# Sums of the down weights moved behind the prompt attention and issued by POOL, with other orders of work around both MLP products, in a one-core decoder layer in split fp32

## The chip, the core and the metric

The kernel runs on one core of one Trainium2 chip. The metric is the device time of one execution in microseconds (us), the median of several runs. The engines are named as in the profile: PE (TensorE, matmuls), DVE (VectorE), ACT (ScalarE), POOL (GpSimd) and SP (the engine that only issues DMAs here).

## The reference

One decoder layer is computed for 1024 prompt tokens with 16 meta tokens ahead of them, and for 8 sequences of 8 new tokens with their caches: L = 1088 output columns, D_MODEL = 1024, D_FF = 4096.

```python
u = _rmsnorm(h, norm_mix)
z = u @ w_in + b_in                      # 1024 -> 6144: pool, conv (2x), q, k, v, three gates
y_a, pool_state = _pool_mixer(a_in, ...) # causal mean pooling, group maps
y_b, conv_state = _conv_mixer(c_in, ...) # GLU, depthwise conv of 31, LayerNorm, silu, product
o, k_state, v_state = _attention_prompt(...) / _attention_sample(...)
y_c = o @ w_attn_out
merged = gates[:, :, 0] * y_a + gates[:, :, 1] * y_b + gates[:, :, 2] * y_c
h = h + merged @ w_out
u2 = _rmsnorm(h, norm_mlp)
h = h + jnp.square(jax.nn.relu(u2 @ w_up)) @ w_down
y = _rmsnorm(h, norm_final)              # and the new pool, conv, key and value states
```

## The kernel before

Every fp32 product is made of three matmuls in a reduced fp32 form: high part by high part, low by high, high by low. A weight tile of 128x1024 is loaded (`wraw`), its high part is rounded off by ACT (`whi`, L90) and the rest made by DVE (`wlo`, L91). Activations lie transposed, with 1088 columns; a tile of output rows is made in three chunks of columns (400, 320 and 368 in the later tiles), 24 matmuls each.

The stages, with their place in the span of the profile: a head to about 77 us; the in-projection, 48 tiles in a loop over `ti` (77 to 724); the products for attention and pooling (724 to 850), the convolution branch (850 to 884) and the merge, W_out (884 to 977); the MLP's up product (977 to 1327) and its down product (1327 to 1679); and the last norm. Both MLP products are made by a scheme with seven products in place of eight (of Strassen's kind), which wants sums of weight blocks and sums of activation blocks.

In the loop over `ti` each chunk is followed by `slot()`, which takes one piece of work from the queue `attq` (attention, norms, loads) and up to two from `dveq` (the 31 convolution taps, each an L444 and an L446 on DVE, among them). Prompt attention runs this way as 64 slices from about 110 to 515 us; then come the sample attention (about 500 to 600 us) and the tiles of the gates. `store()` hands a DMA store to SP at the next slot. Each engine runs its instructions in the order in which the program writes them, so what a queue pops where sets the order.

The pieces that the change touches:

- **Sums of the down weights.** `down_sums` adds and subtracts blocks of `w_down` on POOL (32 times 128x1024, L989), in 8 groups of 4; `sum_load` loads the four blocks of a group (`wd`), and each sum is stored to `sumD` in DRAM, to be read by the down product from 1366 us on. In the kernel before one sum is popped with each of 32 attention slices, the next group's loads go out behind the third sum of a group, and SP issues loads and stores. POOL's other work there is the low part of q (`uq`, L558), on which the attention's score matmuls (`qk`, L569) wait.
- **`tail_slices`** loads and splits the attention's output (`ol`, DVE) for the product that follows.
- **The LayerNorm of the convolution branch** adds four tiles on POOL to `lacc` (L486, L488); PE reads `lacc` (L496, `px<-lacc,ones`) within the gate tiles.
- **Up seam** (977 to 1010 us). The last output rows of W_out are evicted (`h`, L1389), scaled, combined to `t` and split. POOL makes sums of up-weight blocks (`s`, L1266 to L1272), combinations (`t`, L1360, L1361) and the sums of squares of h (`sqa`, L1293, after an ACT square, L1292); from the last `sqa` come the norm's scales, by matmuls with ones (`px<-ones,sqa`, L242), `mv` and `diag` on DVE (L1420, L1421, L248). `start_steps` lists the pieces popped at the first steps of the up product, in that order.
- **Down seam** (1327 to 1355 us). `op_store` stores combined activation blocks (`opT`, `opB`) that the down product loads again (`ld`); the last pair (j = 15) is made while the down product has begun. `W` holds the weight tiles: with `paged` the raw tile and both parts lie in pages of their own, else in rings of two.
- **Last product.** `residual` (L1658, L1657, POOL) adds the old h and the row terms to the output rows; `done` holds that and the sums of squares for the last norm.

## Time and profile before

| | us |
|---|---|
| median of 3 runs (lowest to highest) | 1692.72 (1691.68 to 1692.99) |
| the profiled execution, whole | 1691.97 |
| its span in the trace | 1689.9 |
| PE busy | 1655.2 |
| DVE / ACT / POOL busy | 1091.6 / 747.8 / 513.7 |

The profiled execution spends 2.07 us outside its span. Its time lies between the lowest and the highest of the three runs. The clock that the chip grants PE is given as a share (1.00 is the full 2.4 GHz).

### The profile page before, as it was taken

The page shows a single profiled execution, that of the slowest core. Times are in us where ns is not written, and L with a number is a line of the kernel's source. Part 1 is how long each engine was busy: PE and PEld are TensorE (multiplying, and loading weights), DVE is VectorE, ACT ScalarE, POOL GpSimd, SP SyncE. Part 2 cuts the span into 40 slices and gives each one's busy share as a digit, 9 for nine tenths or more (in the row PEclk, how much of TensorE's full clock was granted, in tenths as well). Part 3 has the DMA queues.
Part 4 walks back from the last instruction along what each step waited for, and adds up shares of the span by engine and source line. Part 5 has one row for each costly group of instructions (what it writes and reads, how often), then busy time and mean ns, then how long its engine had stood idle before and what let it go on. Part 6 is the DMA issues. An engine that isn't in the chain of part 4 may idle for free.

```text
span 1689.9 us, 29160 instructions
## 1 busy us (share of the span) xinstructions
PE 1655.2 (98%) x11552; PEld 1620.4 (96%) x11552; DVE 1091.6 (65%) x1745; ACT 747.8 (44%) x1424; POOL 513.7 (30%) x358
## 2 busy tenths in 40 slices
PE   8999999999999999999999989999999899999997
PEld 7999899998999999999989989999999899999997
DVE  7787878888887666344464575565555644467565
ACT  6536666466665342364243443333333433333341
POOL 1022333133340002212342555555555300013330
PEclk9999999999999999999999999999999999999999
DMA  5255554263545353354243413444444655556552
GB/s 203 65 112 158 156 163 155 72 179 128 160 126 164 108 193 108 101 192 144 79 161 121 152 61 128 143 144 143 144 144 163 250 198 180 183 174 204 203 184 90
DMA packets 124157, 250.79 MB, mean 148 GB/s; under 512 B 33427, under 2 KB 64628, under 8 KB 124020
## 3 DMA queue, kind: packets, MB, share of 16 engines
q1 hardware_dynamic: 124020, 248.92, 44.5%
q8 instruction: 91, 1.49, 0.4%
q14 instruction: 46, 0.38, 0.1%
HBM read 168.52 MB, written 80.36 MB: 147 GB/s over the span
## 4 chain that ended last, share of the span: by engine, by line
PE 77%; DVE 11%; ACT 7%; issue 3%; DMA 1%; POOL 1%; SPq 0%; DVEq 0%; ACTq 0%; POOLq 0%
PE pm L148 9%; PE pm L149 9%; PE pm L150 9%; PE m L1632 6%; PE m L1628 6%; PE m L1630 6%; PE m L1450 6%; PE m L1452 6%; PE m L1453 6%; PE pn L148 3%; PE pn L150 3%; PE pn L149 3%; ACT lg L589 2%; DVE y L446 2%; DVE y L444 2%
## 5 line engine op out<-in xcount | busy, mean ns | idle before, releaser
L148 PE MATMUL pm<-uh,whi 128*128 128x320 f32 (+3 forms) x1008 | 339.0, 336 | 6.5 <-ACT uh L324 6.5
L149 PE MATMUL pm<-ul,whi 128*128 128x320 f32 (+3 forms) x1008 | 333.0, 330 | 0.7 <-DVE ul L325 0.6
L150 PE MATMUL pm<-uh,wlo 128*128 128x320 f32 (+3 forms) x1008 | 332.4, 330 | 0.0
L1628 PE MATMUL m<-oph,whi 128*128 128x272 f32 (+2 forms) x896 | 259.4, 290 | 4.8 <-ACT whi L90 4.8
L1632 PE MATMUL m<-oph,wlo 128*128 128x272 f32 (+2 forms) x896 | 259.0, 289 | 1.2 <-DVE wlo L91 1.2
L1630 PE MATMUL m<-opl,whi 128*128 128x272 f32 (+2 forms) x896 | 258.6, 289 | 0.0
L91 DVE TENSOR_TENSOR wlo<-wraw,whi 128x1024 fp32r<-128x1024 f32 (+1 forms) x127 | 172.6, 1359 | 112.2 <-ACT whi L90 112.2
L90 ACT ACTIVATE whi<-wraw 128x1024 fp32r<-128x1024 f32 (+1 forms) x127 | 130.2, 1026 | 203.6 <-PE m L1630 139.3
L148 PEld LDWEIGHTS pm<-uh,whi 128*128 128x128 f32 x1008 | 191.1, 190 | 7.9 <-ACT uh L324 6.5
L149 PEld LDWEIGHTS pm<-ul,whi 128*128 128x128 f32 x1008 | 191.2, 190 | 3.3 <-DVE ul L325 2.9
L150 PEld LDWEIGHTS pm<-uh,wlo 128*128 128x128 f32 x1008 | 190.9, 189 | 0.2
L1628 PEld LDWEIGHTS m<-oph,whi 128*128 128x128 f32 x896 | 169.4, 189 | 5.1 <-ACT whi L90 5.1
L1632 PEld LDWEIGHTS m<-oph,wlo 128*128 128x128 f32 x896 | 169.3, 189 | 2.0 <-DVE wlo L91 2.0
L1630 PEld LDWEIGHTS m<-opl,whi 128*128 128x128 f32 x896 | 169.5, 189 | 0.0
L444 DVE SCALAR_TENSOR_TENSOR y<-ext,vec,y 128x1024 f32<-128x1024 f32 x120 | 158.7, 1323 | 0.0
L1450 PE MATMUL m<-bch,whi 128*128 128x272 f32 x448 | 130.5, 291 | 3.2 <-DVE mv L1420 2.9
L1450 PE MATMUL m<-bch,wlo 128*128 128x272 f32 x448 | 129.4, 289 | 1.9 <-ACT s L1573 1.1
L1452 PE MATMUL m<-bcl,whi 128*128 128x272 f32 x448 | 130.1, 290 | 0.0
L1453 PE MATMUL m<-bch,whi 128*128 128x272 f32 x448 | 130.0, 290 | 0.0
L558 POOL TENSOR_TENSOR uq<-q,uq 128x128 fp32r<-128x128 f32 x64 | 34.9, 566 | 310.3 <-ACT uq L557 301.6
L1452 PE MATMUL m<-bcl,wlo 128*128 128x272 f32 x448 | 129.0, 288 | 0.0
L1453 PE MATMUL m<-bch,wlo 128*128 128x272 f32 x448 | 128.8, 288 | 0.0
(363 smaller groups left out, 3887.6 us busy)
## 6 DMA issues: line engine op xcount, KB each, us to landing
wraw<-w_in SPq DMA_DIRECT2D x46, 512.0 KB, 4.1
opT<-d SPq DMA_DIRECT2D x64, 272.0 KB, 2.5
ld<-opT SPq DMA_DIRECT2D x32, 544.0 KB, 4.6
wd<-w_down SPq DMA_DIRECT2D x32, 512.0 KB, 5.6
sumD<-wd SPq DMA_DIRECT2D x32, 512.0 KB, 3.5
wraw<-sumD SPq DMA_DIRECT2D x32, 512.0 KB, 3.6
gt<-gD SPq DMA_DIRECT2D x24, 544.0 KB, 4.5
ld<-opB SPq DMA_DIRECT2D x23, 544.0 KB, 4.8
```

Of the source, the lines that this page charges most:

```text
L90: self.nc.scalar.activation(hi, r, AF.Copy)
L91: self.late.append(lambda lo=lo, r=r, hi=hi: self.nc.vector.tensor_tensor(lo, r, hi.bitcast(F32), ALU.subtract))
L148: PE.matmul(ps, lhsT=wh[k], rhs=xh, start=first and i == 0, stop=False)
L149: PE.matmul(ps, lhsT=wh[k], rhs=xl, start=False, stop=False)
L150: PE.matmul(ps, lhsT=wl[k], rhs=xh, start=False, stop=last and i == n - 1)
L444: V.scalar_tensor_tensor(y[:, :NP], e[:, k:k + NP], w, y[:, :NP], ALU.mult, ALU.add)
L1450: PE.matmul(ps, lhsT=wh, rhs=xh, start=first and k == 0, stop=False, skip_group_check=True)
L1452: PE.matmul(ps, lhsT=wh, rhs=xl, start=False, stop=False, skip_group_check=True)
L1453: PE.matmul(ps, lhsT=wl, rhs=xh, start=False, stop=k == 3, skip_group_check=True)
L1628: PE.matmul(ps, lhsT=wh[:, w], rhs=xh[:, r], start=k == 0, stop=False, skip_group_check=True)
L1630: PE.matmul(ps, lhsT=wh[:, w], rhs=xl[:, r], start=False, stop=False, skip_group_check=True)
L1632: PE.matmul(ps, lhsT=wl[:, w], rhs=xh[:, r], start=False, stop=k == 15, skip_group_check=True)
```

## The change

The parts, by number:

1. The sums of the down weights leave the attention slices. They are popped in the tile loop from ti = 31 to 42 by a condition that spreads 32 over 36 chunks; POOL issues the loads and the stores itself, and the next group's loads go out behind the fourth sum. `tail_slices` goes to the front of `attq` at ti = 43.
2. One empty piece of work goes into `attq` ahead of the convolution branch's output loop.
3. W_out's last three chunks take their PSUM banks in another order.
4. `sum_pair(0, 3)` stands ahead of `last_t(1)`.
5. `start_steps`: the two last squares of h are popped with the first and third piece, and their adds are popped by themselves, on DVE, as the seventh and eighth; the norm's scales (`rs[0]`) come after these.
6. `op_store` for j = 15 goes into `attq`, one store a slot.
7. In the last product the weights of mp = 1 to 3 have paged parts and a raw ring of two, and those of mp = 0 rings alone; before, mp = 0 to 2 lay in pages altogether and mp = 3 in rings.
8. `residual(2mp+1, LO)` is queued at the sixth product; the last product's queue holds the sums of squares of rows 1, 3 and 5, the two halves of the last norm's first part, and the sum of squares of row 7.

```diff
+SUM0, SUM1 = 31, 43
...
-        if paged:
+        if paged is True or paged and tag != "wraw":
...
                 if cur:
                     units[n].exps()
-                    sumq.pop(0)()
...
                 attq.extend(sample_slices())
                 attq.append(lambda: wide.append(0))
-                attq.extend(tail_slices())
...
             for b in range(4):
-                SP.dma_start(wdt[g][b], I["w_down"][g // 2, g % 2, b])
+                G.dma_start(wdt[g][b], I["w_down"][g // 2, g % 2, b])
...
                 G.tensor_tensor(t[o], t[a], t[b], op)
-                store(d[n], t[o])
-                if n == 2:
+                G.dma_start(d[n], t[o])
+                if n == 3:
                     sum_load(g + 1)
...
-        if ti == NHEAD:
+        if ti == SUM0:
             sum_load(0)
             for g in range(8):
                 sumq.extend(down_sums(g))
+        if ti == SUM1:
+            attq[:0] = tail_slices()
...
             slot(1, NDVE[0] if attq else NDVE[1])
+            if SUM0 <= ti and sumq and                     len(sumq) * 3 * (SUM1 - SUM0) > 32 * (3 * (SUM1 - ti) - 1 - ci):
+                sumq.pop(0)()
...
+    attq.append(lambda: None)
     for m in range(8):
         wh, wl = weights(WCO + m, 4)
...
-            for t, n in (("px", 3), ("qk", 2), ("qk", 2))]
+            for t, n in (("qk", 2), ("qk", 2), ("px", 3))]
...
+    sum_pair(0, 3)
     last_t(1)
-    sum_pair(0, 3)
...
     def op_store(x, j, t):
-        store(opD[x, j // 2][:, (j % 2) * HL:(j % 2) * HL + HL], t)
+        go = lambda: store(opD[x, j // 2][:, (j % 2) * HL:(j % 2) * HL + HL], t)
+        if j < 15:
+            go()
+        else:
+            attq.append(go)
...
-                                  (n == mp == hf == 0) or (n == NPROD - 1 and mp < 3))
+                                  n == mp == hf == 0 or
+                                  ("out" if n == NPROD - 1 and mp else False))
...
-        def s1():
-            sq_add(7, h7.pop())
-            sq_add(3, h3.pop())
-            comb_split("T3", 3)
-
...
-        return [lambda: comb_split("B22", 3), s1, lambda: comb_split("B21", 3), s3,
-                rs[0], idle, rs[1], s6]
+        sq = []
+
+        def s0(x, h):
+            comb_split(x, 3)
+            sq.append(page("sqt"))
+            A.activation(sq[-1][:, :L], h.pop()[:, :L], AF.Square)
+
+        def add():
+            q = sq.pop(0)
+            V.tensor_tensor(sqa[:, :L], sqa[:, :L], q[:, :L], ALU.add)
+        return [lambda: s0("B22", h3), lambda: comb_split("T3", 3), lambda: s0("B21", h7), s3,
+                idle, add, add, rs[0], idle, rs[1], s6]
...
+            elif n == 5:
+                attq.append(lambda m=2 * mp + 1: residual(m, LO))
...
-    for mp in range(4):
-        attq.extend(done(2 * mp + 1, LO))
-    attq.extend(fin[0] + fin[1])
+    sqs = [lambda m=m: sum_sq(m, LO) for m in (1, 3, 5, 7)]
+    attq.extend(sqs[:3] + fin[0] + fin[1] + sqs[3:])
```

**POOL from the last attention slices to the LayerNorm's first add.** Before, a sum stands behind each pair of `uq`; these are the last two, and the `lacc` adds follow the sample attention's memsets:

```order
L989 TENSOR_TENSOR wd<-wd 128x1024
L558 TENSOR_TENSOR uq<-q,uq 128x128 x2
L989 TENSOR_TENSOR wd<-wd 128x1024
L677 MEMSET sqh 128x1024
L678 MEMSET sql 128x1024
L677 MEMSET sqh 128x1024
L678 MEMSET sql 128x1024
L486 TENSOR_TENSOR lacc<-y 128x1088
L488 TENSOR_TENSOR lacc<-lacc,y 128x1088 x2
```

Now the attention slices hold `uq` alone, and behind the last of them stand eight groups of this kind (the first is shown, `wd` with buffer numbers):

```order
L974 DMA wd_5555<-w_down 128x1024
L974 DMA wd_5556<-w_down 128x1024
L974 DMA wd_5557<-w_down 128x1024
L974 DMA wd_5558<-w_down 128x1024
L988 TENSOR_TENSOR wd_5558<-wd_5557,wd_5558 128x1024
L989 DMA sumD00_5563<-wd_5558 128x1024
L988 TENSOR_TENSOR wd_5557<-wd_5555,wd_5557 128x1024
L989 DMA sumD00_5563<-wd_5557 128x1024
L988 TENSOR_TENSOR wd_5555<-wd_5558,wd_5555 128x1024
L989 DMA sumD00_5563<-wd_5555 128x1024
L988 TENSOR_TENSOR wd_5556<-wd_5556,wd_5555 128x1024
L989 DMA sumD00_5563<-wd_5556 128x1024
```

So POOL has 64 DMAs to issue that it did not have, the first sum of a group reads the block that was asked for last, the loads of a group stand right behind the stores of the one before, and the `lacc` adds stand behind the 32nd sum. In PE's order the first matmul out of `lacc` stands 96 matmuls of the tiles (four chunks) later than before.

**POOL at the up seam.** Before (one pair's last sums and the next pair's first):

```order
L1360 TENSOR_TENSOR t_10212<-u 128x544
L1361 TENSOR_TENSOR t_10212<-u,t_10107 128x544
L1272 TENSOR_TENSOR s_10088<-wra 128x512
L1293 TENSOR_TENSOR sqa<-sqa,sqt 128x1088 x2
L1266 TENSOR_TENSOR s_10354<-wraw 128x512
L1268 TENSOR_TENSOR s_10354<-s_10354,wraw 128x512
```

Now:

```order
L1276 TENSOR_TENSOR s_10088<-wra 128x512
L1364 TENSOR_TENSOR t_10213<-u 128x544
L1365 TENSOR_TENSOR t_10213<-u,t_10107 128x544
L1270 TENSOR_TENSOR s_10350<-wraw 128x512
L1272 TENSOR_TENSOR s_10350<-s_10350,wraw 128x512
```

The last sum of the first pair has moved ahead of the two combinations, and the two adds of squares have left POOL.

**SP at the down seam.** Before:

```order
L1521 DMA ld<-opT_10240 128x1088
L222 DMA opB_10270<-cb 128x544
L222 DMA opB_10254<-cb 128x544
L222 DMA opT_10238<-d_14010 128x544
L222 DMA opT_10246<-d_14010 128x544
L222 DMA opT_10262<-d_14012 128x544
L222 DMA opT_10278<-d_14012 128x544
L1521 DMA ld<-opT_10241 128x1088
L61 DMA wraw<-w_down 128x1024
L1521 DMA ld<-opT_10242 128x1088
```

Now:

```order
L1530 DMA ld<-opT_10240 128x1088
L1530 DMA ld<-opT_10241 128x1088
L223 DMA opB_10270<-cb 128x544
L62 DMA wraw<-w_down 128x1024
L1530 DMA ld<-opT_10242 128x1088
L223 DMA opB_10254<-cb 128x544
L62 DMA wraw<-w_down 128x1024
L1530 DMA ld<-opT_10243 128x1088
L223 DMA opT_10238<-d_14010 128x544
L62 DMA wraw<-w_down 128x1024
```

The six stores stood in a row ahead of a weight load; now each stands between loads.

## Rows read from the trace of the kernel before

**Rows 1.** The page's first part: busy time of each engine, its share of the span, and instructions.

```profile
PE 1655.2 (98%) x11552; PEld 1620.4 (96%) x11552; DVE 1091.6 (65%) x1745; ACT 747.8 (44%) x1424; POOL 513.7 (30%) x358
```

**Rows 2.** What PE waited for, over the span: us in total, times, longest.

```profile
PE m L1628 <- ACT whi L90: 4.8, 2, 4.0
PE m L1450 <- DVE mv L1420: 2.9, 1, 2.9
...
PE qk L569 <- POOL uq L558: 1.0, 2, 0.8
PE qk L569 <- ACT uq L557: 0.9, 1, 0.9
```

**Rows 3.** Windows over the attention slices: the stretch and its length, then busy us (and instructions) of PE, PE's weight loads, DVE, ACT and POOL, then the granted clock, DMA share and GB/s.

```profile
160.00:180.00 20.00, 18.68 (x108) 16.88 (x107) 15.42 (x37) 13.51 (x33) 4.45 (x5) 0.91 0.29 93
...
200.00:340.00 140.00, 139.05 (x926) 131.93 (x925) 116.61 (x238) 85.00 (x225) 42.37 (x31) 1.00 0.42 128
...
420.00:440.00 20.00, 18.94 (x129) 17.15 (x129) 18.31 (x39) 10.05 (x29) 8.42 (x6) 1.00 0.37 102
440.00:520.00 80.00, 79.45 (x535) 74.95 (x535) 65.84 (x134) 52.86 (x143) 28.96 (x22) 1.00 0.43 141
```

**Rows 4.** One sum on POOL and DVE's instructions beside it, in order of time (start, us), then PE's wait that followed.

```profile
156.91 3.36 POOL L989 TENSOR_TENSOR wd<-wd 128x1024 f32<-128x1024 f32 x1
157.96 2.39 DVE L446 SCALAR_TENSOR_TENSOR y<-exts,vec,y 128x64 f32<-128x64 f32 x1
164.19 1.28 ACT L589 ACT_TABLE_LOAD   x1 [4.07 <-issue]
170.41 0.38 PE L569 MATMUL qk<-kh,uq 64*128 64x256 f32 x2 [0.92 <-ACT uq L557]
```

**Rows 5.** All instructions of three lines: shortest, median and longest duration in ns, first and last start in us.

```profile
L446 DVE SCALAR_TENSOR_TENSOR y<-exts,vec,y x120: 265/280/2446, 86.9 to 650.4; 128x64 f32<-128x64 f32 x120
L989 POOL TENSOR_TENSOR wd<-wd x32: 2369/3370/3405, 115.2 to 500.1; 128x1024 f32<-128x1024 f32 x32
L558 POOL TENSOR_TENSOR uq<-q,uq x64: 450/461/2011, 111.8 to 499.7; 128x128 fp32r<-128x128 f32 x64
```

**Rows 6.** The DMAs of the sums: the issue on SP of a load and of a store (ns, as in rows 5), and the loads' time from issue to landing.

```profile
L975 SPq DMA_DIRECT2D wd<-w_down x32: 327/383/1038, 56.9 to 447.4; - x32
DMA to landing us min/median/max: 3.5/5.6/10.0
L222 SPq DMA_DIRECT2D sumD<-wd x32: 320/326/1385, 117.6 to 503.8; - x32
```

**Rows 7.** The gate tiles: two windows, in the columns of rows 3, two of `tail_slices`' eight splits on DVE, then the LayerNorm's adds on POOL, and PE's matmuls out of them.

```profile
515.00:685.00 170.00, 170.00 (x1063) 168.11 (x1062) 110.33 (x221) 63.58 (x137) 12.56 (x6) 1.00 0.43 142
620.00:640.00 20.00, 20.00 (x121) 20.00 (x120) 20.00 (x26) 8.63 (x12) 0.00 (x0) 1.00 0.43 149
617.65 2.49 DVE L154 TENSOR_TENSOR ol<-ld,oh 128x1088 fp32r<-128x1088 f32 x2 [0.46 <-ACT oh L153]
657.27 3.45 POOL L486 TENSOR_TENSOR lacc<-y 128x1088 f32<-128x1088 f32 x1 [150.12 <-DVE pts L464]
660.80 6.15 POOL L488 TENSOR_TENSOR lacc<-lacc,y 128x1088 f32<-128x1088 f32 x2
L496 PE MATMUL px<-lacc,ones x6: 432/484/485, 678.5 to 688.5; 128*128 128x384 f32 x4, 128*128 128x320 f32 x2
```

**Rows 8.** Windows at the up seam and in the up product behind it, in the columns of rows 3.

```profile
980.00:1010.00 30.00, 24.89 (x174) 24.09 (x172) 23.00 (x29) 12.10 (x20) 18.26 (x10) 0.89 0.18 61
1020.00:1300.00 280.00, 280.00 (x2237) 280.00 (x2236) 162.10 (x159) 86.04 (x146) 159.39 (x106) 1.00 0.43 146
```

**Rows 9.** Single instructions at the up seam: start, us, and in brackets the idle time ahead with what ended it.

```profile
987.60 0.63 ACT L153 ACTIVATE whi<-s 128x512 fp32r<-128x512 f32 x1 [3.43 <-POOL s L1272]
989.82 5.52 POOL L1293 TENSOR_TENSOR sqa<-sqa,sqt 128x1088 f32<-128x1088 f32 x2 [2.25 <-ACT sqt L1292]
995.50 2.07 PE L242 MATMUL px<-ones,sqa 128*128 128x1 f32 x18
1003.53 0.57 PE L1450 MATMUL m<-bch,whi 128*128 128x272 f32 x1 [2.86 <-DVE mv L1420]
```

**Rows 10.** One window at the down seam, in the columns of rows 3.

```profile
1345.00:1355.00 10.00, 5.54 (x26) 5.00 (x26) 4.86 (x4) 4.12 (x4) 0.00 (x0) 0.66 0.96 366
```

**Rows 11.** SP and ACT at the down seam, in order of time.

```profile
1335.33 0.80 SPq L222 DMA_DIRECT2D opB<-cb  x2
1336.22 6.54 SPq L222 DMA_DIRECT2D opT<-d  x4
1343.28 0.44 SPq L61 DMA_DIRECT2D wraw<-w_down  x1
1348.26 1.06 ACT L90 ACTIVATE whi<-wraw 128x1024 fp32r<-128x1024 f32 x1 [8.27 <-DMA wraw<-w_down]
```

**Rows 12.** The last product's start: a window in the columns of rows 3, and DVE, POOL and PE in order of time.

```profile
1630.00:1635.00 5.00, 3.64 (x28) 3.31 (x26) 3.91 (x5) 2.52 (x4) 1.98 (x2) 1.00 0.11 41
1623.70 3.52 DVE L91 TENSOR_TENSOR wlo<-wraw,whi 128x1024 fp32r<-128x1024 f32 x2
1633.91 0.41 PE L1628 MATMUL m<-oph,whi 128*128 128x288 f32 x1 [0.80 <-ACT whi L90]
```

More of the change, by code (lines that the diff above doesn't have):

```diff
@@ L1288, in hybrid_trunk_kernel, with sq_add @@
     sqa = page("sqa")
-    def sq_add(m, t):
+    def sq_add(m, t, eng=G):
         q = page("sqt")
         A.activation(q[:, :L], t[:, :L], AF.Square)
-        G.tensor_tensor(sqa[:, :L], sqa[:, :L], q[:, :L], ALU.add)
+        eng.tensor_tensor(sqa[:, :L], sqa[:, :L], q[:, :L], ALU.add)
     def scaled(m):
```

## Prediction

> **What bounds the kernel now.** I read the page's first part, PE's waits, and windows along the span. PE is busy for 1655.2 of 1689.9 us [rows 1], so no other engine's load can bound the whole: DVE is at 65%, POOL at 30%. The change leaves the matmuls as they are in number and shape. What it can win is time in which PE waits or runs at a lower clock; what it can lose is a new wait of PE. PE's waits [rows 2] name the places: the down seam (`m L1628 <- ACT whi`, 4.8 us), the up seam (`mv`, 2.9 us, the longest there) and score matmuls of the attention that wait for `uq`. A wait isn't the whole loss, since the clock falls behind it. I therefore take the loss of a seam from the number of matmuls in its window against the pace of the up product, 280 us for 2237, which is 0.125 us each [rows 8].
>
> **Part 1a: the sums leave the attention slices.** Over four stretches [rows 3] PE is idle for 1.32 + 0.95 + 1.06 + 0.55 = 3.9 us, and at a granted clock of 0.91 the 20 us from 160 lose another 1.8: 5.7 us. What the sums have to do with it shows in one place [rows 4]: a sum starts on POOL at 156.91 and ends at 160.27; DVE's L446 starts at 157.96 and lasts until then, 2.39 us, where its median is 0.28 [rows 5]. DVE is 2.1 us late, ACT's exponentials behind it start with 4.07 us of idle time, and a score matmul waits 0.92. 32 such delays make 67 us of DVE, in stretches where DVE is busy for 83% (116.6 of 140) [rows 3]. With the sums gone, POOL has only `uq` there, and SP neither 32 loads nor 32 stores. **Gain 6 us.** The bounds are 0 (the waits come from ACT's table loads in any case) and 12 (twice what the windows show, because ends of matmuls are modelled and short gaps don't show as idle).
>
> The Trainium skill ("SBUF — State Buffer", section "SBUF: two separate sides") says that DVE and POOL share one pair of ports under an exclusive lock, held for a whole instruction, the loser standing still. The trace agrees: the 64-column L446 lasts exactly as long as the sum. By this rule the 67 us don't vanish, but move with the sums to the gate tiles.
>
> **Part 1b: what the sums cost in the gate tiles.** There PE is busy throughout (170.00 of 170 us), DVE for 110.3, POOL for 12.6 [rows 7]. POOL can start at 500.2, behind its last `uq` (499.7 plus 0.46) [rows 5]. It must be done when the LayerNorm's adds begin. PE reads `lacc` at 678.5 now; four chunks later, 96 matmuls at 170/1063 = 0.16 us, is 693.9. The adds take 3.45 + 6.15 with their gaps, 9.7 us [rows 7]. So the 32nd sum is due at 684.2, 184 us after the start, or 23.0 us per group of four. A group's chain is: four issues of loads, the landing of the last, four sums, four issues of stores, hence 8x + L + 4t, where x is what one issue holds POOL. t lies between 2.37 (a sum alone) and 3.37 (the median beside a busy DVE) [rows 5]; DVE is less busy here than in the attention, 65% against 83%, so I take 2.9. L lies between 3.5 and 5.6 us [rows 6]; I take 4.5, since DMA is no busier there. The four memsets stand behind the second group's loads and so inside their landing. x is not in the trace, as POOL issues no DMA before. From below it is what SP needs, 0.33 to 0.38 us. From above it would be a whole landing, 5.6 us for a load; but SP is free 0.4 us after its issue, so that an issuer need not stay with the transfer. The nearest rows are SP's slowest issues, 1.04 and 1.39 us [rows 6]. I take 0.9, between SP's median and its slowest store. Then a group takes 7.2 + 4.5 + 11.6 = 23.3 us, eight take 186, and the last sum is 2 us late; PE waits that long at `lacc`. With x = 0.38 it is done 31 us early, with x = 1.39 27.2 × 8 = 218 us, 34 late.
>
> DVE in the gate tiles: 110 us of work and up to 67 of delay in 170 us. It becomes tight only where taps run back to back, as from 620 to 640 (20.00 of 20 us busy) [rows 7]; at 5.7 us a sum some six fall into such a 32 us, 12 us of delay, while `tail_slices`' eight splits of 1.25 us, 10 us of DVE, leave it for later. So `wlo` comes late by a few us at most: 2 us, between 0 and 5. The stores of the first groups can hold back pages that the sample attention wants; with three PSUM banks ahead of PE's evictions I price it within the same bounds. **Loss 4 us**, between 0 and the rival's price below.
>
> **Parts 3, 4 and 5: the up seam.** From 980 to 1010 there are 174 matmuls, 18 of them one-column ones that take 2.07 us [rows 8, 9]. At the pace above the other 156 need 19.5 us, so 30 − 19.5 − 2.07 = 8.4 us are lost. The steps: a weight sum (`s L1272`) comes late from POOL, so ACT's `whi` is idle for 3.43 us and PE behind it; two adds of squares hold POOL for 5.52 us and lock DVE's splits beside them; 18 matmuls for the scales, `mv` and `diag` then stand ahead of DVE's split and PE waits 2.86 us, and the clock of the window is 0.89 [rows 9, 8]. The change makes the sum ahead of the combinations, puts the adds on DVE two pieces later, and the scales behind them, in steps of the up product where DVE is busy for 162 of 280 us [rows 8]. The two adds cost DVE some 2.5 us in place of POOL, and `diag` stays as it was; both lie then beside PE's steps (16 pairs of 7 in 350 us, 3.1 us each), whose operands are made a step or more ahead. The bank order lets the first matmul of the second step go without the third eviction. I take 7 of the 8.4 back: **gain 7**, between 4 and 8.4. If that cover were gone, what is late next is the norm's scales, worth 2.9 us.
>
> **Part 6: the down seam.** From 1345 to 1355 26 matmuls run, 3.25 us of work: 6.75 us lost [rows 10]. SP issues the four `opT` stores at 1336.22 and sits in them for 6.54 us, because they wait for POOL's combinations; the weight load behind them goes out at 1343.28, lands as ACT starts at 1348.26, after 8.27 us of idle time [rows 11]. With the stores spread, that load goes out behind the first `opB` store, at about 1336, 7 us earlier, and, at the same 5 us, lands about 1341, before PE ran dry at 1345. The stores that wait for POOL can still hold up a later load, but only one store stands ahead of each. **Gain 6.6**, between 5 and 6.75.
>
> **Parts 7 and 8: the last product.** PE loses 1.36 us from 1630 to 1635, where ACT's `whi` follows DVE's tail of `wlo`, 3.52 us for two beside POOL's residuals [rows 12]. The residuals now come a product earlier. Against it a ring of two raw tiles has to feed short halves. **Gain 1.5**, between −2 and 2. Part 2 puts nothing into any engine: 0.
>
> **The sum.** 6 − 4 + 7 + 6.6 + 1.5 = 17.1 us. Against the profiled execution, 1691.97 in all, that gives 1674.9; this execution lies within the runs of the median, so I leave it there: 1675.
>
> **Rivals.** (a) *POOL's issues are dear, and `lacc` comes late: slower.* At x = 1.39, the slowest store issue of SP, the chain is 34 us late; PE stands still for it, and 1674.9 + 32 = 1707. It decides from the point where the lateness eats the 21 us of the other terms and 2 us more for DVE: 8x = (184 + 19)/8 − 16.1, so x = 1.16. For it speaks that 64 issues stand in one chain with no load ahead of its use; against it that SP's median is a third of that. At x = 2 the price would be 73 us (1746).
> The Trainium skill ("DMA: Bandwidth & Descriptors", section "Anatomy of one DMA — SWDGE (gpsimd) path") gives about 2.0 us as the fixed cost of a DMA from POOL, completion included; no run here shows it yet. Were all of it POOL's, the sum would be that last price. The same skill ("SBUF — State Buffer", the section named above) warns that POOL can't write its descriptors while DVE holds the ports, which would lengthen x where taps run back to back.
> (b) *The chain is partly late* (x of 1.0 to 1.16): 24.1 to 25.4 us a group, 9 to 19 us late: 1682 to 1692, faster still or the same.
> (c) *Little comes of it:* the attention's waits belong to ACT and the seams' waits are taken over by the next in line (a load behind the `opB` stores, the split behind `diag`): 1 + 3 + 1 − 4 = 1 us, 1691.
>
> **How the numbers follow.** About 0.2% (3.4 us) is what a measurement of this kernel can tell from no change: 1689.3 to 1696.1 is the same. The forecast case, sums hidden or late by a few us (1664 to 1684): 0.58. Rival (b) up to 1689: 0.17, faster too. Rival (c) and the end of (b): 0.08, the same. Rival (a): 0.17, from 1696 to 1746. So faster 0.75, same 0.08, slower 0.17. The low end is the forecast with the attention at 12 and the gate tiles at no cost, 1691.97 − 12 − 7 − 6.6 − 1.5 = 1665, less one for the up seam: 1664. The high end is 1696, beyond which most of (a) is left out.
>
> **What would show it.** In the profile after: attention windows with PE busy throughout and L446 at most 0.3 us before 500; a first `lacc` matmul with no wait (right), or with a wait of several us for POOL (rival a or b); the length of POOL's DMA issues, which is x; L446 of 2.4 us among the gate tiles (the lock moved along); in the up seam no wait for `mv` and a window with some 220 matmuls; at 1345 no wait for `whi`, the weight load some 7 us earlier. The prediction is wrong if the issue on POOL takes over 1.2 us, or if a wait of the same length stands behind one that has gone.

## The result, and the profile after

| | before | after |
|---|---|---|
| median | 1692.2 us (1691.55 to 1692.99, 4 runs) | 1711.78 us (1710.07 to 1717.32, 4 runs) |
| ratio to before, 95% interval | | 1.0121 [1.0097, 1.0145] |
| profiled execution, span | 1691.97, 1689.9 us | 1712.49, 1710.5 us |
| mean granted clock | 0.993 | 0.987 |

Two executions ran far beyond all others of their kernels and are left out: one of `no_dma` (second experiment, 4465.61 us, the profiled one, so that the same kernel was run again as `lock_alone`) and one of `pool_att` (tenth, 3324.14 us).

The change makes the kernel 1.2% slower. 1675 was forecast with a range of 1664 to 1696: the time lies outside it, on the other side of no change.

The page's first part: PE's busy time is that of before [rows 1], in a span 20.6 us longer, so the loss is idle PE. POOL has 18 us more, its DMA issues among them.

```profile
PE 1655.2 (97%) x11552; PEld 1622.8 (95%) x11552; DVE 1100.6 (64%) x1747; ACT 750.5 (44%) x1426; POOL 531.9 (31%) x420
```

Both programs run 11552 matmuls, so the loss is put to its place by the start of the matmul of the same number in both traces. Each row is what a stretch of before adds to that difference. The stretches between these add under 1 us each. The head, before 120 us, gives -1.6 here; it differs by as much between executions of kernels that are alike there.

| stretch of before, us | forecast | after |
|---|---|---|
| attention slices, 120 to 520 | -6 | -14.8 |
| sample attention, 520 to 560 | together with the next | +19.9 |
| gate tiles, 560 to 724 | +4 for both | +21.7 |
| up seam, 977 to 1010 | -7 | -7.1 |
| down seam, 1340 to 1355 | -6.6 | -6.9 |
| last product, 1630 to 1680 | -1.5 | +9.9 |

What PE waited for, in the columns of [rows 2]. The seams' two waits are gone; in their place stand `sqk` (the sample attention's scores), `pm` and `px` (the gate tiles), `diag` and `whi` (the last product).

```profile
PE pm L151 <- DVE wlo L92: 9.1, 7, 4.0
PE sqk L723 <- DVE skk L709: 8.1, 5, 4.4
PE px L497 <- POOL lacc L489: 5.7, 1, 5.7
PE sqk L722 <- ACT skk L708: 4.0, 2, 2.2
PE px L254 <- DVE diag L249: 3.4, 2, 1.7
PE m L1642 <- ACT whi L91: 2.2, 2, 1.8
```

Six windows, in the columns of [rows 3]. In 200 to 340 PE starts 951 matmuls where before started 926: at the 140/951 = 0.147 us that one takes here, that is 3.7 us won, though the idle time there was 0.95 us. In the sample attention and at the LayerNorm's start (520 to 560, 680 to 720) PE stands for 8.9 and 12.0 us at a clock of 0.84; in before it was busy for 170.00 of 170 us from 515 to 685 [rows 7]. DMA, 0.43 busy there in before [rows 7], is now 0.69 to 0.79. The up seam (1005 to 1035) has 231 matmuls in 30 us, where it had 174 [rows 8], and the down seam (1362 to 1372) has no gap left [rows 10].

```profile
200.00:340.00 140.00, 140.00 (x951) 134.31 (x950) 99.73 (x240) 85.86 (x227) 12.27 (x23) 1.00 0.23 64
520.00:560.00 40.00, 31.12 (x166) 30.02 (x165) 28.32 (x62) 9.92 (x32) 21.73 (x18) 0.84 0.79 273
560.00:640.00 80.00, 79.89 (x499) 78.04 (x498) 69.46 (x97) 23.62 (x55) 40.99 (x33) 1.00 0.70 242
...
680.00:720.00 40.00, 27.99 (x144) 26.17 (x143) 18.06 (x14) 14.51 (x20) 22.37 (x12) 0.84 0.69 249
...
1005.00:1035.00 30.00, 28.93 (x231) 28.52 (x231) 26.86 (x28) 15.13 (x25) 17.80 (x10) 1.00 0.30 105
1362.00:1372.00 10.00, 10.00 (x82) 10.00 (x82) 4.56 (x4) 4.64 (x5) 0.00 (x0) 1.00 0.90 313
```

**The chain on POOL.** All instructions of the sums (ns, first and last start, as in [rows 5]), then POOL's idle time ahead of them with its releasers (us, times) and the loads' time to landing. The chain runs from 482.1 to 704.0, 222 us, 27.7 a group. An issue takes 0.53 or 0.58 us, and a store waits 0.41 for its sum. The largest part that isn't addition is the wait for loads, 64 us, 8.0 a group; some 19 us go to pages that the sample attention holds (`str`, `ssm`).

```profile
L974 POOL DMA_DIRECT2D wd<-w_down x32: 530/535/727, 482.1 to 674.1; - x32
L988 POOL TENSOR_TENSOR wd<-wd x32: 2340/2420/5817, 491.5 to 700.6; 128x1024 f32<-128x1024 f32 x32
L989 POOL DMA_DIRECT2D sumD<-wd x32: 573/578/588, 494.2 to 703.4; - x32
...
  DMA wd<-w_down: 64.0, 8
  POOL wd L988: 12.7, 32
  PE str L747: 10.7, 1
  DVE ssm L732: 8.3, 1
...
DMA to landing us min/median/max: 4.6/7.1/15.1
```

**The sample attention.** In order of time, DVE, PE, POOL, SP and ACT of after. From 515.45 to 528.03 POOL makes four sums, of which the last three are shown. DVE's L442 and L443, 0.80 and 0.31 us at their medians, last 3.41 and 2.98, and L447, 0.28, lasts 2.36; they end 0.55, 0.06 and 0.09 us behind the sum beside them. `skk` comes behind them, and PE has waited 4.41. Then POOL asks for a group's four blocks, 2 MB, from 529.01 to 531.54; SP asks for a tile of 128 KB at 531.16, and it lands as ACT starts at 539.19, 8.0 us later.

```profile
518.33 3.41 DVE L442 TENSOR_SCALAR y<-ext,vec 128x1024 f32<-128x1024 f32 x1
518.80 2.39 POOL L988 TENSOR_TENSOR wd<-wd 128x1024 f32<-128x1024 f32 x1
521.66 2.98 DVE L443 TENSOR_SCALAR y<-exts,vec 128x64 f32<-128x64 f32 x1
522.19 2.39 POOL L988 TENSOR_TENSOR wd<-wd 128x1024 f32<-128x1024 f32 x1
525.59 2.44 POOL L988 TENSOR_TENSOR wd<-wd 128x1024 f32<-128x1024 f32 x1
525.76 2.36 DVE L447 SCALAR_TENSOR_TENSOR y<-exts,vec,y 128x64 f32<-128x64 f32 x1
528.50 0.53 PE L723 MATMUL sqk<-skk,sqh 128*128 128x192 f32 x1 [4.41 <-DVE skk L709]
529.73 1.08 POOL L974 DMA_DIRECT2D wd<-w_down  x2 [0.18 <-issue]
531.16 0.39 SPq L699 DMA_DIRECT2D skv<-ckT  x1
539.19 0.42 ACT L708 ACTIVATE skk<-skv 128x256 fp32r<-128x256 f32 x1 [3.13 <-DMA skv<-ckT]
```

**The LayerNorm's start.** POOL, ACT and PE. The last group's loads land 14.75 us after the last issue, and the 32nd store ends at 703.96. The adds follow, and PE goes on at 712.70. ACT stands for 17.83 us ahead of that: `oh`, the first half of the split that `tail_slices` make, wants a page of the sums. PE's evictions (`zs`) queue behind it on ACT.

```profile
689.43 3.34 POOL L988 TENSOR_TENSOR wd<-wd 128x1024 f32<-128x1024 f32 x1 [14.75 <-DMA wd<-w_down]
...
703.98 2.56 POOL L487 TENSOR_TENSOR lacc<-y 128x1088 f32<-128x1088 f32 x1
706.62 6.03 POOL L489 TENSOR_TENSOR lacc<-lacc,y 128x1088 f32<-128x1088 f32 x2
707.55 2.11 ACT L154 ACTIVATE oh<-ld 128x1088 fp32r<-128x1088 f32 x2 [17.83 <-DMA sumD<-wd]
712.70 1.65 PE L497 MATMUL px<-lacc,ones 128*128 128x384 f32 x2 [5.67 <-POOL lacc L489]
```

**The down seam.** SP and ACT, to be read with [rows 11]. The weight load goes out right behind the first `opB` store. Less the 17.9 us by which PE is late just ahead of this place, that is 1336.2, where it was 1343.28.

```profile
1353.67 0.32 SPq L223 DMA_DIRECT2D opB<-cb  x1
1354.08 0.38 SPq L62 DMA_DIRECT2D wraw<-w_down  x1
1358.33 1.06 ACT L91 ACTIVATE whi<-wraw 128x1024 fp32r<-128x1024 f32 x1 [0.44 <-DMA wraw<-w_down]
```

### The profile page after: what moved, and what is told of

Same layout as the page of the kernel before. It is cut to its first block, busy times and chain, and to the rows that moved or that the text cites. A ratio compares the mean times of both kernels' runs of the same rounds, so it can differ in the third digit from the quotient of the medians.

```text
span 1710.5 us, 29128 instructions
## 1 busy us (share of the span) xinstructions
PE 1655.2 (97%) x11552; PEld 1622.8 (95%) x11552; DVE 1100.6 (64%) x1747; ACT 750.5 (44%) x1426; POOL 531.9 (31%) x420
## 4 chain that ended last, share of the span: by engine, by line
PE 51%; POOL 4%; DVE 4%; DMA 3%; issue 3%; ACT 2%; DVEq 0%; POOLq 0%; ACTq 0%
PE m L1646 6%; PE m L1644 6%; PE m L1642 6%; PE m L1454 6%; PE m L1457 6%; PE m L1456 6%; POOL wd L988 3%; DMA wd<-w_down 3%; PE pm L151 2%; PE pm L149 2%; PE pm L150 2%; PE pn L151 2%; PE pn L149 2%; PE pn L150 2%; DVE wlo L92 1%
## 5 line engine op out<-in xcount | busy, mean ns | idle before, releaser
L92 DVE TENSOR_TENSOR wlo<-wraw,whi 128x1024 fp32r<-128x1024 f32 (+1 forms) x127 | 178.8, 1409 | 87.5 <-ACT whi L91 87.5
L445 DVE SCALAR_TENSOR_TENSOR y<-ext,vec,y 128x1024 f32<-128x1024 f32 x120 | 160.8, 1340 | 0.0
```

The lines of the kernel that those rows point to most:

```text
L92: self.late.append(lambda lo=lo, r=r, hi=hi: self.nc.vector.tensor_tensor(lo, r, hi.bitcast(F32), ALU.subtract))
L445: V.scalar_tensor_tensor(y[:, :NP], e[:, k:k + NP], w, y[:, :NP], ALU.mult, ALU.add)
```

## The experiments

Three causes were in question for the +41.6 us from 520 to 724: the **transfers** (POOL's loads and stores crowd out the sample attention's small loads, and the chain waits for its own), the **lock** (the additions stop DVE), and the **pages** (the sums hold pages that others want). Stretches are those of the table above.

**1. The additions left out.** Against after. The stores write the raw blocks, so that the 64 transfers stay.

```diff
-                G.tensor_tensor(t[o], t[a], t[b], op)
```

> The kernel after, with the 32 additions on POOL left out and all 64 transfers kept (raw blocks are stored as sums, so the output isn't the layer's). Theory (chain and transfers): a group is some 8 us of landing and 5 of issues, the chain ends by 620, so the tail waits for no page and 19 us come back, while the sample attention keeps the part of its 20 us that late landings make, 5 to 12: 1680 to 1688. Rival (lock alone): with no instruction of POOL to lock DVE out, both losses go: 1670 to 1674. If transfers alone make the loss, 1700 or more.

1687.3 us (8 runs), 0.9973 [0.996, 0.9987]. The gate tiles lose 1.7 in place of 21.7, as the chain is without the 84.5 us of sums and ends at 640.9. The sample attention still loses 16.1, with no addition in the program: PE waits for ACT's `skk`, ACT for a load, and the loads of L699 take 5.0 us at the median, where before had 2.5. The rows of PE's waits and of that landing, and last the landing in before:

```profile
PE sqk L722 <- ACT skk L708: 9.3, 2, 5.0
...
DMA to landing us min/median/max: 2.3/5.0/7.0
...
DMA to landing us min/median/max: 2.0/2.5/4.2
```

**2. The additions without the transfers.** Against after. One group's four blocks are loaded and added eight times over; nothing is stored, and the down product reads raw blocks, so the result's values change but the work behind 724 us keeps its size. Both names are this kernel; the numbers are those of the second.

```diff
         if g < 8:
+            if g:
+                wdt[g] = wdt[g - 1]
+                return
...
-                G.dma_start(d[n], t[o])
...
-        return sumD[a, mp, hf] if a in "S1S2S3S4" else I["w_down"][mp, hf, ABLK[a]]
+        return I["w_down"][mp, hf, ABLK.get(a, 2)]
```

> The kernel after, with the sums' transfers left out: one group's four loads, then all 32 sums on POOL over the same four pages, no stores; the down product reads raw weight blocks in their place, so the output isn't the layer's. Theory (chain and transfers): the loss of 40 us in the gate tiles comes from POOL's chain, which waits 64 us for its loads, holds pages until its stores land and fills the DMA engines. Without transfers the 32 sums end within some 90 us of their start, the stretch from ti 40 to 47 loses nothing (19 us back) and the sample attention loses at most half of its 20: 1680 to 1688. Rival (lock alone): DVE stands still beside the sums whether they have transfers or not, so that both stretches lose what they lose now: 1705 to 1712.

> Again the kernel after without the sums' transfers but for one group's loads (output not the layer's), because the one run had a profile far off the others. With no load to wait for, POOL adds 32 times in a row from about 484 us. If the transfers alone make the loss of the sample attention (16 of 20 us were there without sums): 1677 to 1686. If the lock does it too: POOL holds DVE for some 67 us within 100, the sample attention starves, 1700 to 1730, as the one time of 1729 has it.

1723.82 us (2 runs), 1.0191 [1.017, 1.0211]. With no transfers between them the 32 additions stand back to back from 493 to 584, on top of the sample attention, and that loses 53.1 us; the gate tiles lose 3.8. The window 520 to 560 shows what the lock alone does: DVE and POOL both busy for 39 of 40 us, DVE with 30 instructions where after had 62, and PE stands.

```profile
PE sqk L723 <- DVE skk L709: 33.0, 6, 15.1
...
520.00:560.00 40.00, 17.08 (x72) 16.59 (x73) 39.80 (x30) 1.76 (x6) 39.14 (x16) 0.67 0.22 67
```

So the transfers alone cost the sample attention 16.1 us, where after lost 19.9 with both, and the additions alone, packed closer than in after, cost 53.1. Either is enough, and the two don't add.

**3. Parts 7 and 8 undone.** Against after: the last product's raw rings and its order as before.

```diff
-                                  n == mp == hf == 0 or
-                                  ("out" if n == NPROD - 1 and mp else False))
+                                  (n == mp == hf == 0) or (n == NPROD - 1 and mp < 3))
...
-            elif n == 5:
-                attq.append(lambda m=2 * mp + 1: residual(m, LO))
...
-    sqs = [lambda m=m: sum_sq(m, LO) for m in (1, 3, 5, 7)]
-    attq.extend(sqs[:3] + fin[0] + fin[1] + sqs[3:])
+    for mp in range(4):
+        attq.extend(done(2 * mp + 1, LO))
+    attq.extend(fin[0] + fin[1])
```

> The kernel after with parts 7 and 8 undone (weight rings and order of the last product as before). Theory: the last product, which lost 10 us from 1630 on, gets them back, 1700 to 1703. Rival: the loss there follows from the shifted start (other transfers in flight, the clock), then 1710 to 1713.

1706.12 us (1701.79 to 1707.96), 1.008 [1.0058, 1.0102]. This lies between the two forecasts. In the trace the last product is back at +0.1 and the other stretches are as in after, to 1.2 us; the profiled execution is the fastest of the four, 4.3 us under their median.

**4. Parts 2 to 6 alone.** Against after: the third experiment's edit, and the sums in the attention slices with SP's transfers.

```diff
                 if cur:
                     units[n].exps()
+                    sumq.pop(0)()
...
+                attq.extend(tail_slices())
...
-                G.dma_start(wdt[g][b], I["w_down"][g // 2, g % 2, b])
+                SP.dma_start(wdt[g][b], I["w_down"][g // 2, g % 2, b])
...
-                G.dma_start(d[n], t[o])
-                if n == 3:
+                store(d[n], t[o])
+                if n == 2:
...
-        if ti == SUM0:
+        if ti == NHEAD:
...
```

> The kernel before with parts 2 to 6 alone (parts 1, 7 and 8 undone). Theory: the two seams' gains, 7.1 and 7.0 us by the traces, stand by themselves: 1677 to 1680. Rival: they are due to the other state in which the shifted parts arrive there (weights loaded further ahead after long stalls), then 1685 to 1693.

1677.14 us (1676.51 to 1677.8), 0.9911 [0.9891, 0.9932]. The up seam gives 7.0 and the down seam 6.9; 120 to 724 is as before, to 0.1 us.

**5. The sums on DVE, in the attention slices.** One line against the fourth: the attention's gain, if the lock is its cause, without the move.

```diff
-                G.tensor_tensor(t[o], t[a], t[b], op)
+                V.tensor_tensor(t[o], t[a], t[b], op)
```

> Parts 2 to 6 alone as in seams_only, and the 32 sums in the attention slices as before with SP's transfers, but added on DVE in place of POOL. In the kernel before the attention lost 14.6 us against the kernel after, which has no sums there. Theory (the lock): a sum on POOL holds DVE up by 2.07 us, a sum on DVE costs it some 1.2 us and leaves POOL to uq, so a good half of the 14.6 comes back: 1665 to 1672. Rival: the attention loses what DVE is given in work, and 38 us more of it in order ahead of the softmax cost as much as the lock: 1676 to 1684.

1664.53 us (1663.55 to 1665.72), 0.9838 [0.9822, 0.9855]: the fastest of all, 27 us under before and 47 under after. The attention gains 14.6, as much as in after, and the stretches behind it lose nothing. A sum takes 1.22 us on DVE, less than the 2.1 us by which a sum on POOL held up DVE (2.39 less L446's median of 0.28 [rows 4, 5]); and with the additions off POOL L447 never lasts over 0.47 us. In the trace of before the lock acts nearly every time: beside 28 of the 32 sums on POOL DVE's instructions last 2.1 to 2.4 us over their medians. Another reading would be that `uq` stood behind the sums in POOL's own order. It doesn't fit: in before POOL had been idle for at least 3.6 us ahead of every pair of `uq`.

```profile
L990 DVE TENSOR_TENSOR wd<-wd x32: 1217/1219/1226, 117.4 to 491.2; 128x1024 f32<-128x1024 f32 x32
...
L447 DVE SCALAR_TENSOR_TENSOR y<-exts,vec,y x120: 265/277/474, 87.1 to 636.1; 128x64 f32<-128x64 f32 x120
```

**6. Pages or the chain's end?** Against after: `tail_slices`, whose `oh` wanted a page, queued three tiles later.

```diff
-        if ti == SUM1:
+        if ti == 46:
```

> The kernel after with tail_slices at ti = 46 in place of 43; all else the same. Theory: the 17 us from 680 on come from oh and ld, which get pages that POOL's sums still hold (ACT stood 17.8 us for a store of a sum to land, and the evictions behind it). Three tiles later the chain, which ended at 703, is done; the stretch loses the wait of lacc alone, 5 to 8 us, and total 1697 to 1705. Rival: it is lacc that is late in any case and the page wait lies beside it: 1709 to 1713.

1726.48 us (2 runs), 1.0206 [1.0186, 1.0227]; the gate tiles lose 39.4. Neither forecast came: the wait for a page is gone and the loss is larger. But the move changes more than that wait: PE's first matmul out of `lacc` stands 144 matmuls earlier in this kernel's order, and PE meets it while the chain still runs. The chain itself ends at 697.71, 6.3 us earlier than in after. In after six loads of `tail_slices` go out from 671.40 to 680.61 beside the last group's, DMA is 1.03 busy from 680 to 690, and the first sum waits 14.75; here it waits 9.06 and DMA is 0.57 busy. So the chain's end is enough for the loss, and part of its lateness in after goes with `tail_slices`' loads. What ACT's wait for a page costs by itself this run doesn't show.

```profile
PE px L497 <- POOL lacc L489: 27.1, 1, 27.1
```

**7. Part 7 undone by itself.** Against after: the first hunk of the third experiment alone.

> The kernel after with part 7 undone (weights of the last product as before), part 8 kept. Theory: the raw ring of two feeds the short halves of the last product too slowly; 8 to 10 us come back from 1630 on: 1702 to 1704. Rival: the order of sums of squares and norms (part 8) makes the loss: 1710 to 1713.

1712.82 us (2 runs), 1.0126 [1.0105, 1.0146]: no change to after. In its trace the last product loses 5.0 in place of 9.9, the two stretches from 520 to 724 lose 3 more.

**8. and 9. Parts 8 and 7, each beside parts 2 to 6.** Against the fourth: part 8 (the last two hunks of the third experiment, the other way round), then part 7 (its first hunk).

> seams_only (parts 2 to 6) with part 8 added: residuals a product earlier, sums of squares and the last norm's first part in the new order. Undoing both parts 7 and 8 gave the last product's 10 us back in the trace, undoing part 7 alone 5. Theory: part 8 costs 4 to 6 us from 1630 on, 1681 to 1684. Rival: parts 7 and 8 cost only together, then 1676 to 1678.

1683.28 us (10 runs, 1680.87 to 1689.43), 0.9954 [0.9942, 0.9965]: 6 us over the fourth. The first halves of the last norm go through DVE ahead of the last row's square. PE waits 1.7 us for `diag` twice, where it did once in the fourth, and 2.2 us more for `whi` and `wlo`.

> seams_only (parts 2 to 6) with part 7 added: raw ring of two and paged parts for the last product's weights, with the residuals' old order. Theory: part 7 by itself costs 0 to 2 us: 1677 to 1680. Rival: the ring of two feeds the short halves too slowly, 5 us or more: 1682 to 1687.

1681.82 us (4 runs), 0.9945 [0.9929, 0.996]: 4.7 us over, near the rival's price and not the theory's. PE waits for ACT's `whi` at the last product's start, where three weight loads sit 10.76 us in SP (6.91 in the fourth). They wait for DVE's `wlo`, behind which a raw tile of the ring of two comes free:

```profile
1595.06 10.76 SPq L62 DMA_DIRECT2D wraw<-w_down  x3
...
1623.73 0.61 PE L1640 MATMUL m<-oph,whi 128*128 128x288 f32 x1 [4.42 <-ACT whi L91]
```

**10. POOL's issues in the attention slices.** Against the fourth: loads and stores by `G.dma_start`, the next group's loads at n = 3 as in after; the additions stay on POOL.

> seams_only with the sums' 64 transfers issued by POOL, the sums still on POOL in the attention slices. Theory: the issuing engine costs little where the sums lie 12 us apart and each load is asked for a sum ahead; POOL spends 0.55 us more per transfer ahead of uq: 1676 to 1682. Rival: transfers from POOL are slow in themselves and hold up uq and the softmax: 1685 or more.

1674.24 us, 0.9895 [0.9877, 0.9913]; the attention gains 4.6. Issuing by POOL, with the loads a sum later, is a small gain here and not a loss. What of it belongs to the issuer and what to the order isn't parted, and the lock is still there: L447 lasts up to 2.43 us.

**11. A chain with more time.** Against the third: the sums popped from tile 20, among the last attention slices, so that a group has some 34 us.

```diff
-SUM0, SUM1 = 31, 43
+SUM0, SUM1 = 20, 43
```

> The kernel after with parts 7 and 8 undone (1706 by itself) and the sums popped from ti = 20 to 42, one in some 8.5 us of PE's work in place of 4.4, all else the same. Theory: the chain needs 25 to 28 us for a group, so at 34 us a group it no longer falls behind, lacc and the tail wait for nothing (17 us back), the sample attention meets half as many transfers (5 to 12 back), and the last attention slices lose some 4 to a lock again: 1680 to 1690. Rival: any sum from POOL among the gate tiles costs what it costs now, half of the 40 us stay and the attention's loss comes on top: 1695 or more.

1692.52 us (10 runs), 1.001 [1.0, 1.002]. The gate tiles lose 1.8 in place of 20.5: the chain ends at 622 and nobody waits for it. The sample attention still loses 17.7, where 5 to 12 us were to come back. Two rows, in order of time: one load, issued among a group's four, takes 10.5 us to land.

```profile
528.66 0.44 SPq L699 DMA_DIRECT2D skv<-ckT  x1
...
539.28 0.42 ACT L708 ACTIVATE skk<-skv 128x256 fp32r<-128x256 f32 x1 [4.77 <-DMA skv<-ckT]
```

**12. Both gains of the attention together.** Against the tenth: the line of the fifth.

> dve_att (sums on DVE in the attention slices) with the transfers issued by POOL in place of SP. If SP's queue costs the attention the 3 us that pool_att won, and the lock the other 10 to 11, they add up: 1661 to 1663. Rival: POOL's store now waits for DVE ahead of uq, which takes the place of the lock: 1666 to 1672. If what pool_att won was the same lock, moved by POOL's own issues: 1664 to 1666.

1666.59 us (1664.52 to 1667.69), 0.9848 [0.9832, 0.9865]. The attention gains 12.1, less than with SP's transfers: the two don't add.

## Why the prediction was wrong

**The attention (1a): right in kind, too small.** The lock was the cause, as the fifth experiment shows, which takes only the POOL additions away and gets 14.6 of the 14.8 us. The failed step is the bound: "12 (twice what the windows show)". Idle time and clock showed 5.7 us, and the stretch gained 14.8. The matmuls started per window show what idle time doesn't: 3.7 us from 200 to 340, where 0.95 was idle. A matmul's record lasts 0.32 us there at the mean and the next one starts 0.15 us behind it, so that a delay shorter than the difference leaves no idle time. The prediction used that measure for the seams, whose terms came out within 0.3 us, and not here. One reading in it is loose: L446 lasts until the sum's end, to 0.08 us, having begun 1.05 us behind its start [rows 4], and not "exactly as long as the sum".

**The gate tiles and the sample attention (1b): the step that failed.** Of x the prediction said 0.9; it measured 0.53 for a load and 0.58 for a store, 0.99 with the 0.41 us that a store waits, so an issue's price was met or better. t was 2.64 at the mean, beside 2.9. L failed: 4.5 was taken from SP's loads, "since DMA is no busier there", and 8.0 a group was measured. SP's loads too go out four in a row in before (from 446.01 to 447.84), so the row of four is no difference. DMA is: it was 0.43 busy in the gate tiles before, and the chain's own transfers, which the prediction left out of that figure, bring it to 0.69 to 0.79. Pages add 19 us to the chain. So 27.7 a group came in place of 23.3. The chain began 18 us earlier than assumed, and PE, whose lead of 16 us was lost in the sample attention, came to the tiles behind 640 later by 4.1; so 206 us were there for the chain, and it took 222.

The larger miss is one sentence: "three PSUM banks ahead of PE's evictions I price it within the same bounds". It thought of pages alone. The sample attention is a chain of small loads, splits and scores, which the prediction priced at nothing of its own, and 19.9 us were lost there. POOL's bursts make its loads late (PE waits up to 5.0 us in the first experiment), and POOL's sums lock the DVE that splits them (up to 15.1 us in the second). The prediction looked for DVE's tight place at 620 to 640, where DVE has no gap. The loss came from 520 to 560, where DVE is busy for 28.32 of 40 us and PE waits for its next result. The Trainium skill ("SBUF — State Buffer", section "SBUF: two separate sides") has the rule of the lock. The trace agrees in one thing: L447 begins at 525.76, behind the sum that POOL began at 525.59, and ends 0.09 us behind it. It differs in another: by the rule the one that starts first has the ports, and L442 and L443 begin, by the record, 0.47 and 0.53 us ahead of their sums and are held all the same. Why, no run here shows. The prediction concluded from the rule that the delay moves along, and let only 4 us follow from it.

**Rival (a)** gave 1707, near the 1711.8 that came, but not by its mechanism: it put the lateness on an issue of 1.16 us or more, and none took over 0.73. `lacc` was late by about 15 us (the adds end at 712.65; PE, 4.1 us behind before at 640, would have been there at the forecast's 693.9 + 4.1 = 698.0), and the sample attention gave the other 20. The Trainium skill's figure of about 2.0 us for a DMA from POOL ("DMA: Bandwidth & Descriptors", section "Anatomy of one DMA — SWDGE (gpsimd) path") isn't what POOL is held for: these rows show 0.53 to 0.58, and the rest as a landing of at least 4.6 us that the next instruction needn't wait for.

**The last product (7 and 8): wrong in sign.** −1.5 was forecast, with "a ring of two raw tiles has to feed short halves" as the risk, at 2 us at most. Undoing both gives 5.7 us between medians (10.7 between the profiled executions, 9.8 of it in the last product). Beside parts 2 to 6 alone, part 7 costs 4.7 us by the medians and part 8 6.1 (3.3 and 3.5 in the last product of the traces). Part 8 moved the norm's pieces ahead of the last row's square on DVE, which the prediction didn't follow. With part 8 in, PE's waits are the same in after, the seventh and the eighth experiment: `diag` 3.4 us, `whi` 2.1 to 2.2, `wlo` 1.8, and the seventh loses 5.0 by them. The other 4.9 of after's 9.9 stand in the clock (0.4 + 1.3 + 3.4 us by the rows below). It falls below 1.00 twice there, where PE has been idle for half of the 5 us from 1645 and where it has waited 1.70 us for `diag` at 1680.86; from 1680 to 1685 it is 0.50, the lower of its two levels. In the seventh's trace the same stretches stay at 1.00. Three windows of after, in the columns of [rows 3]:

```profile
1645.00:1650.00 5.00, 2.46 (x14) 2.04 (x13) 3.89 (x7) 2.62 (x4) 0.00 (x0) 0.92 0.12 15
1650.00:1655.00 5.00, 5.00 (x31) 5.00 (x30) 2.05 (x5) 0.84 (x2) 0.00 (x0) 0.74 0.80 269
...
1680.00:1690.00 10.00, 9.14 (x55) 9.18 (x56) 4.14 (x13) 0.83 (x2) 0.00 (x0) 0.66 0.09 31
```

**The seams (3 to 6): right**, 7.1 and 6.9 us for 7 and 6.6, with the two waits gone that were named and the weight load 7.1 us earlier. Parts 2 to 6 weren't undone one by one, so which of them gives the up seam's 7 is not shown.

**The sum.** The attention gives 8.8 more than forecast, the stretch behind it costs 37.6 more, the last product 11.4 more, the head, the seams and the rest give 2.6 more: 37.6 − 8.8 + 11.4 − 2.6 = 37.6, and 1712.5 − 1674.9 is 37.6.

**Open.** How the 20 us of the sample attention divide between burst and lock in after: each is enough without the other, and no kernel had both thinned out there. Spreading a group's loads there was not tried. What part 7 adds in the last product when 8 is in isn't settled either: the seventh experiment's trace is without the fall of the clock there, but its median is that of after. And why issuing by POOL gained 4.6 us in the attention slices, with the lock still there, is open.

## What to carry to other kernels

Moved work takes its transfers and its lock along, so look first at what is most sensitive in the place that it goes to: here a short chain of small loads lost more than the stretch where DVE had no gap. Count matmuls per window, not only idle time, when you ask what a stall behind a pipelined engine costs. Before moving work off a stretch, ask whether another engine does it in less time than its neighbour loses to it: one word in one line, the additions on DVE, gave all of the attention's gain.

## What the runs showed of the hardware

- A DMA issue held POOL for 0.53 us (load) and 0.58 us (store) of 128x1024 fp32, and no more than 0.73 in any of 64.
- A burst of four 512 KB loads put a 128 KB load issued behind it from 2.5 us (median before) to 8.0 us until landing, and one issued among the four to 10.5 in the eleventh experiment. Burst and load were issued by different engines, POOL and SP.
- The same addition of two 128x1024 fp32 tiles took 1.22 us on DVE, in each of 32 (fifth experiment), and 2.34 to 5.82 on POOL (after).
- The lock lengthened DVE's instructions, short and long, until 0.06 to 0.55 us behind the end of the sum beside them: 0.80 to 3.41, 0.31 to 2.98 and 0.28 to 2.36 us in one run of four sums. Two of the three had begun, by the record, about 0.5 us ahead of the sum.
- The granted clock fell to 0.50 for 5 us behind a wait of PE of 1.70 us in the last product of after; behind the same wait it stayed at 1.00 in the seventh experiment.
